# Three engines held to one written order in the first stage of a two-layer transformer step

## The chip, the cores and the metric

The kernel runs on one core of a Trainium2 chip. The metric is the device time of one execution, in microseconds. The text says PE for TensorE, DVE for VectorE, ACT for ScalarE, POOL for GpSimd and SP for SyncE, as the profile does; each takes its own instructions in their order in the program.

## The reference

Two layers (neighbourhood attention, then a gated linear recurrence), each with a feed-forward network, on 640 tokens (512 latent, 128 context) of width 1024. Each sub-layer begins with an RMS norm that is modulated by a conditioning vector; the change lies in the first one and in the first product behind it.

```python
def _adaln(cond, w_mod, b_mod):
    m = jax.nn.silu(cond) @ w_mod + b_mod
    return jnp.split(m, N_MOD, axis=-1)

def _modulate(x, g, shift, scale):
    return _rms_norm(x, g) * (1 + scale[:, None, :]) + shift[:, None, :]

xm_l = _modulate(lat, norm_g[i, 0], sh1_l, sc1_l)   # with cond = c; context tokens: cond = c_ctx
q_l, k_l, v_l = _qkv(xm_l, attn_w_qkv[j])
```

## The kernel before

Activations lie with their features on partitions: eight tiles `k` = 0 to 7 of 128 features by 640 tokens (`KT` = 8). A product in float32 accuracy is made of three matmuls in a faster format: each operand is split into a high part (a cast on ACT) and a low part (value less high part, on DVE), and high·high, low·high and high·low are summed in one bank of PSUM. `split` (L1061 to L1063) does this for a tile, `unit` (L166 to L181) for a weight tile that it also loads.

The first stage is `start`. SP issues its loads in one queue: eight tiles of `x`, 16 tiles of the first modulation weights (`sw`, 512 KB each: group `g` of two tiles `k`, scale `j` = 1 or shift `j` = 0, half `h`), and in between the query and the key weights of the first head pair (`raw` from `wqk`, L313). Behind them follow the value weights (`raw` from `wv`, L170), the conditioning vectors spread over all partitions (`csb`, L1127) and more.

Then, in this order of dependence:

- The statistic: ACT squares, DVE sums to `ssq`, `moment` lets PE sum over partitions (L390), DVE and POOL make the inverse root (L392, L394), DVE writes it on diagonals (L399) and PE spreads it over all partitions (L402), ACT copies it to `rsb` (L403), the latent 512 columns and the context 128 apart.
- The adaLN vectors, `vectors(g)`: PE multiplies a piece (L327, 16 passes for one `g` and `j`), DVE (`j` = 1) or ACT (`j` = 0) copies the row (L328), four small matmuls select the columns (L334) and four small DVE instructions finish the factors `A` and shifts `B` of two tiles (L339, L340).
- The scaling, `scaled(k, A, B)`. An even tile: DVE multiplies by `A` and `rsb` (L350), ACT adds `B` into the high part (L351), DVE makes the low part (L352), each for the latent and the context columns. An odd tile: POOL multiplies it by `rsb` beforehand (L369), ACT scales and shifts it (L348), then `split`.
- The products, `products(k)`: 12 matmuls (L362 to L364) on two weights (query, key) and two chunks of 320 tokens, into four banks that collect all eight `k`.

What runs behind the stage starts with `qk(0, ...)`, which empties those four banks, and `vq(0, ...)`, whose matmuls L228 to L230 take the value weights (split by L180 on ACT and L181 on DVE).

The order on each engine isn't that of the code: a scheduler with its own estimates of durations chooses it under the dependences, so instructions of several groups `g`, and of what follows the stage, lie mixed.

Of the kernel before, what the change touches and what calls it, by code (L numbers as in the profile page):

```python
# [9 lines left out]
F32 = mybir.dt.float32  # L10
F32R = mybir.dt.float32r
# [114 lines left out]
class _Step:  # L126
# [161 lines left out]
    def start(self, hi, lo, sp, big):  # L288
# [14 lines left out]
        for g in range(KT // NB):  # L303
            for j in (1, 0):
                for h in range(2):
                    w = self.t([P, 4, n], F32, f"sw{g}{j}{h}", 1, sp)
                    nc.sync.dma_start(w, self.i["wm0"][j, g, h])
                    parts[g, j, h] = w
            if g == 1:
                raws = []  # L310
                for f in (0, KT):
                    raw = self.t([P, KT, P], F32, "raw", 3)
                    nc.sync.dma_start(raw, self.i["wqk"][f])  # L313
                    raws.append(raw)
# [3 lines left out]
            if k:  # L318
                nc.vector.tensor_tensor(ssq, ssq, q, ALU.add)

        def vectors(g):
            pm = {j: self.ps("sp") for j in (1, 0)}
            row = idle[:, g % 2 * 2 * n:g % 2 * 2 * n + 2 * n]
            for j in (1, 0):
                for h in range(2):
                    for k4 in range(4):
                        nc.tensor.matmul(pm[j][32 * k4:32 * k4 + 32, 0:n], csp[:, 4 * h + k4], parts[g, j, h][:, k4], start=(h == 0), stop=(h == 1))  # L327
                (nc.vector.tensor_copy if j else nc.scalar.copy)(row[:, j * n:j * n + n], pm[j][:, 0:n])  # L328
            out = []
            pt = self.ps("tp")  # L330
            for j in (1, 0):
                for kb in range(NB):
                    q = NB * j + kb
                    nc.tensor.matmul(pt[:, 2 * q:2 * q + 2], row[:, q * P:q * P + P], sel, start=True, stop=True)  # L334
            for kb in range(NB):
                k = g * NB + kb
                A = self.t([P, 2], F32, "a0", 4, sp)
                B = self.t([P, 2], F32, "b0", 4, sp)
                nc.vector.tensor_scalar(A, pt[:, 2 * (NB + kb):2 * (NB + kb) + 2], b1[:, k:k + 1], self.col("ng00", k), ALU.add, ALU.mult)  # L339
                nc.vector.tensor_scalar(B, pt[:, 2 * kb:2 * kb + 2], self.col("bsh", k), None, ALU.add)  # L340
                out.append((k, A, B))
            return out

        def scaled(k, A, B):
            for s, a, b in _pieces(0, NTOK):
                v = self.x[:, k, a:b]
                if k % 2:
                    nc.scalar.activation(v, v, AF.Identity, scale=A[:, s:s + 1], bias=B[:, s:s + 1])  # L348
                else:
                    nc.vector.scalar_tensor_tensor(v, v, A[:, s:s + 1], self.rsb[:, a:b], ALU.mult, ALU.mult)  # L350
                    nc.scalar.activation(hi[:, k, a:b], v, AF.Identity, bias=B[:, s:s + 1])  # L351
                    nc.vector.scalar_tensor_tensor(lo[:, k, a:b], v, B[:, s:s + 1], hi[:, k, a:b].bitcast(F32), ALU.add, ALU.subtract)  # L352
            if k % 2:
                self.split(hi[:, k, 0:NTOK], lo[:, k, 0:NTOK], self.x[:, k, 0:NTOK])

        acc = [[self.pg(), self.pg()], [self.pg(), self.ps("op")]]

# [5 lines left out]
                    nc.tensor.matmul(ps, wl[:, k], hi[:, k, s], start=False, stop=False)  # L363
                    nc.tensor.matmul(ps, wh[:, k], lo[:, k, s], start=False, stop=(k == KT - 1))  # L364

        vec = vectors(0)
        self.moment(ssq, sp)
        for k in range(1, KT, 2):
            nc.gpsimd.tensor_tensor(self.x[:, k], self.x[:, k], self.rsb, ALU.mult)  # L369
        for g in range(1, KT // NB + 1):  # L370
            todo = vec
            for t in todo:
                scaled(*t)
            if g < KT // NB:
                vec = vectors(g)
            if us is None:
                us = []
                for raw in raws:
                    u = [self.t([P, KT, P], F32R, m, 3) for m in ("whi", "wlo")]
                    self.split(*u, raw)  # L380
                    us.append(u)
            for t in todo:
                products(t[0])
        return acc

    def moment(self, ssq, sp):
# [5 lines left out]
        nc.vector.tensor_scalar(v, ps[:, 0:NT], 1.0 / D, EPS, ALU.mult, ALU.add)  # L392
        r = self.t([P, 8], F32, "rs", 2)[:, 0:NT]
        nc.gpsimd.tensor_tensor(r, v, self.mhalf.broadcast_to([P, NT]), ALU.pow)  # L394
        dg = self.t([P, NT, P], F32, "dg", 1, sp)
        self.rsb = self.t([P, NTOK], F32, "rsb", 1, sp)
        for s, a, b in _pieces(0, NTOK):
            j, m = a // P, (b - a) // P
            nc.vector.tensor_tensor(dg[:, j:j + m], self.ident.unsqueeze(1).broadcast_to([P, m, P]), r[:, j:j + m].unsqueeze(2).broadcast_to([P, m, P]), ALU.mult)  # L399
            ps = self.ps("sp" if s == 0 else "tp")  # L400
            for q in range(j, j + m):
                nc.tensor.matmul(ps[:, (q - j) * P:(q - j) * P + P], self.ones, dg[:, q], start=True, stop=True)  # L402
            nc.scalar.copy(self.rsb[:, a:b], ps[:, 0:b - a])  # L403

    def square(self, k, t0, t1):
        nc = self.nc
# [658 lines left out]
    def lru_gate(self, f, hi, lo, lp):  # L1065
# [152 lines left out]
```

## Time and profile before

| | |
|---|---|
| median of 3 runs | 1559.95 us (1559.09 to 1560.55) |
| the profiled execution: time | 1561.15 us |
| its span, first to last instruction | 1559.4 us |
| PE, DVE, ACT, POOL busy | 1491.8, 1079.1, 717.9, 208.9 us |
| DMA, mean over the span | 121 GB/s |

A timeline row gives the start, the length, the engine, the line, the operation, the tile written and the tiles read, a count of merged instructions, and in brackets the idle time before it with what ended it. A row of a group gives the count, then busy time and mean duration, then the idle time before its instructions. PEld are weight loads, SPq is a DMA issue. The pages count times from the span's start.

### The profile page before, as it was taken

The numbers are of one execution on the slowest core, as the hardware profiler recorded it, in microseconds if no ns is written. First come the engines' busy times: TensorE is split into PE (matmuls) and PEld (weight loads), VectorE is DVE, ScalarE is ACT, GpSimd is POOL, SyncE is SP. The second block draws the span as 40 slices with busy tenths as digits, with TensorE's granted clock in tenths as the row PEclk, the third lists the DMA queues.
The fourth block names the chain that finished last, engine by engine and source line by source line (L and its number), as shares of the span: only waits on it lengthen the run. The fifth ranks groups of instructions, "written<-read, shape, count | busy, mean of one in ns | idle before, by whom it ended". The sixth has DMA issues, their size and how long they took to land.

```text
span 1559.4 us, 26024 instructions
## 1 busy us (share of the span) xinstructions
PE 1491.8 (96%) x10303; PEld 1444.5 (93%) x10303; DVE 1079.1 (69%) x2042; ACT 717.9 (46%) x1326; POOL 208.9 (13%) x230
## 2 busy tenths in 40 slices
PE   5999999989999999999999999969999999999996
PEld 3899999879999999999999887869999999999996
DVE  5678688859899996444446489875876665556545
ACT  4676667654332123212334499754634342524231
POOL 2111122100111110000000000000132323232300
PEclk9999999989999999999999999989999999999997
DMA  9545555536566663222223112134242231313111
GB/s 377 157 131 170 159 167 168 145 118 200 176 191 188 209 207 100 73 82 82 62 83 113 62 62 68 55 108 153 68 132 80 70 109 55 109 55 108 55 55 68
DMA packets 69753, 188.25 MB, mean 121 GB/s; under 512 B 7792, under 2 KB 23296, under 8 KB 69504
## 3 DMA queue, kind: packets, MB, share of 16 engines
q1 hardware_dynamic: 57824, 144.49, 29.2%
q0 software_dynamic: 11520, 41.95, 8.8%
q8 instruction: 81, 1.33, 0.3%
q14 instruction: 40, 0.33, 0.1%
q10 hardware_dynamic: 288, 0.16, 0.0%
HBM read 171.09 MB, written 8.92 MB: 115 GB/s over the span
## 4 chain that ended last, share of the span: by engine, by line
PE 82%; ACT 7%; DVE 7%; issue 3%; DMA 1%; POOL 0%; DVEq 0%; ACTq 0%; POOLq 0%
PE mm L213 13%; PE mm L212 13%; PE mm L214 13%; PE mx L212 5%; PE mx L213 5%; PE mx L214 5%; PE mx L825 3%; PE mx L827 3%; PE mx L826 3%; PE op L671 2%; PE tp L595 2%; PE mc L825 1%; PE mc L826 1%; PE mc L827 1%; PE mm L228 1%
## 5 line engine op out<-in xcount | busy, mean ns | idle before, releaser
L212 PE MATMUL mm<-big,whi 128*128 128x320 f32 (+2 forms) x1251 | 389.9, 314 | 15.3 <-ACT big L1062 9.2
L213 PE MATMUL mm<-big,whi 128*128 128x320 f32 (+2 forms) x1251 | 391.4, 313 | 4.3 <-DVE big L1063 4.0
L214 PE MATMUL mm<-big,wlo 128*128 128x320 f32 (+2 forms) x1251 | 390.6, 313 | 0.0
L212 PEld LDWEIGHTS mm<-big,whi 128*128 128x128 f32 x1251 | 237.1, 190 | 18.4 <-ACT big L1062 10.0
L213 PEld LDWEIGHTS mm<-big,whi 128*128 128x128 f32 x1251 | 238.1, 190 | 6.3 <-DVE big L1063 5.4
L214 PEld LDWEIGHTS mm<-big,wlo 128*128 128x128 f32 x1251 | 237.7, 190 | 1.1
L242 DVE SCALAR_TENSOR_TENSOR mprod<-mraw,csb 128x1024 f32<-128x1024 f32 x160 | 195.4, 1221 | 7.2 <-DMA mraw<-in_wm 6.5
L180 ACT CAST whi<-raw 128x1024 fp32r<-128x1024 f32 (+1 forms) x87 | 90.2, 1037 | 131.3 <-PE mm L213 77.2
L462 DVE SCALAR_TENSOR_TENSOR x<-mm,G,x 128x192 f32<-128x192 f32 (+3 forms) x211 | 84.6, 434 | 91.2 <-PE mm L214 90.2
L181 DVE TENSOR_TENSOR wlo<-raw,whi 128x1024 fp32r<-128x1024 f32 (+1 forms) x87 | 105.9, 1218 | 29.1 <-ACT whi L180 26.1
L214 PE MATMUL mm<-big,wlx 128*128 128x320 f32 (+3 forms) x362 | 112.3, 310 | 0.0
L213 PE MATMUL mm<-big,whx 128*128 128x320 f32 (+3 forms) x362 | 112.1, 310 | 0.0
L212 PE MATMUL mm<-big,whx 128*128 128x320 f32 (+3 forms) x362 | 112.1, 310 | 0.0
L238 POOL DMA_DIRECT2D mraw<-in_wm x80 | 43.2, 540 | 381.4 <-DVE mprod L242 268.4
L212 PE MATMUL mx<-big,whi 128*128 128x320 f32 (+3 forms) x285 | 90.1, 316 | 0.9 <-DVE big L680 0.9
L213 PE MATMUL mx<-big,whi 128*128 128x320 f32 (+3 forms) x285 | 89.6, 314 | 0.0
L214 PE MATMUL mx<-big,wlo 128*128 128x320 f32 (+3 forms) x285 | 89.4, 314 | 0.0
L432 POOL TENSOR_TENSOR rs<-var,mhalf 128x3 f32<-128x3 f32 (+1 forms) x8 | 7.7, 961 | 569.1 <-DVE var L430 569.1
L180 ACT CAST whx<-raw 128x1024 fp32r<-128x1024 f32 (+1 forms) x39 | 40.0, 1027 | 89.5 <-PE mm L213 53.3
L212 PE MATMUL mx<-big,whx 128*128 128x320 f32 (+3 forms) x246 | 76.5, 311 | 0.0
L213 PE MATMUL mx<-big,whx 128*128 128x320 f32 (+3 forms) x246 | 76.3, 310 | 0.0
L214 PE MATMUL mx<-big,wlx 128*128 128x320 f32 (+3 forms) x246 | 76.3, 311 | 0.0
(300 smaller groups left out, 3691.4 us busy)
## 6 DMA issues: line engine op xcount, KB each, us to landing
raw<-in_gu SPq DMA_DIRECT2D x88, 512.0 KB, 3.5
mraw<-in_wm POOLq DMA_DIRECT2D x80, 512.0 KB, 4.0
raw<-in_dn SPq DMA_DIRECT2D x24, 512.0 KB, 3.6
sw<-in_wm SPq DMA_DIRECT2D x16, 512.0 KB, 10.1
raw<-in_wqk SPq DMA_DIRECT2D x16, 512.0 KB, 3.7
raw<-in_wi SPq DMA_DIRECT2D x16, 512.0 KB, 3.5
raw<-in_dn SPq DMA_DIRECT2D x16, 448.0 KB, 3.3
raw<-in_wv SPq DMA_DIRECT2D x8, 512.0 KB, 4.0
```

The source lines that it names most:

```text
L180: nc.scalar.copy(hi, raw)
L181: nc.vector.tensor_tensor(lo, raw, hi.bitcast(F32), ALU.subtract)
L212: nc.tensor.matmul(ps, hi[:, k], xhi[:, k, s], start=(k == 0), stop=False)
L213: nc.tensor.matmul(ps, hi[:, k], xlo[:, k, s], start=False, stop=False)
L214: nc.tensor.matmul(ps, lo[:, k], xhi[:, k, s], start=False, stop=(k == nk - 1))
L238: nc.gpsimd.dma_start(w, self.i["wm"][l * 6 + j - 2, f])
L242: nc.vector.scalar_tensor_tensor(prod, w, 1.0, self.csb[:, s], ALU.mult, ALU.mult, accum_out=out[:, s, f:f + 1])
L462: self.nc.vector.scalar_tensor_tensor(xs, ps[:, a - t0:b - t0], G[:, s, f:f + 1], xs, ALU.mult, ALU.add)
L595: nc.tensor.transpose(tp[:, j * P:j * P + P], s[:, j * P:j * P + P], self.ident)
L825: nc.tensor.matmul(ps, hi[:, k], xh[:, k], start=start and k == 0, stop=False, skip_group_check=not start)
L826: nc.tensor.matmul(ps, hi[:, k], xl[:, k], start=False, stop=False, skip_group_check=not start)
L827: nc.tensor.matmul(ps, lo[:, k], xh[:, k], start=False, stop=(k == KH - 1), skip_group_check=not start)
```

## The change

- `vectors(g)` falls into `piece(g, j)` (one piece and the copy of its row) and `select(g)`; `moment` ends with the diagonals, and `spread(s)` does the rest for one of the two column ranges.
- The query and key weights are loaded behind the first four `sw` tiles instead of eight. Their split falls into `weight(j)` (ACT) and `rest(j)` (DVE).
- `scaled` takes an even and an odd tile together and issues the steps of both in a fixed sequence.
- `in_order` adds dependences without a wait, so that PE, DVE and ACT each take the stage's instructions in the order of the code. Instructions from behind the stage may still be put in between.

```diff
-            if g == 1:
+            if g == 0:
                 raws = []
                 for f in (0, KT):
                     raw = self.t([P, KT, P], F32, "raw", 3)
...
+            lat, ctx = (0, a0, a1), (1, p0, p1)
+            for step, part in ((gain, lat), (gain, ctx), (whole, lat), (high, lat), (high, ctx), (whole, ctx), (low, lat), (low, ctx)):
+                step(*part)
+            self.split(hi[:, m, 0:NTOK], lo[:, m, 0:NTOK], self.x[:, m, 0:NTOK])
...
-        vec = vectors(0)
-        self.moment(ssq, sp)
-        for k in range(1, KT, 2):
-            nc.gpsimd.tensor_tensor(self.x[:, k], self.x[:, k], self.rsb, ALU.mult)
-        for g in range(1, KT // NB + 1):
-            todo = vec
-            for t in todo:
-                scaled(*t)
-            if g < KT // NB:
-                vec = vectors(g)
...
-            for t in todo:
-                products(t[0])
+        def pieces(g):
+            piece(g, 1)
+            piece(g, 0)
+
+        def ready(g):
+            scaled(*select(g))
...
+        us = []
+        with self.in_order(mybir.EngineType.PE, mybir.EngineType.DVE, mybir.EngineType.Activation):
+            piece(0, 1)
+            self.moment(ssq, sp)
+            piece(0, 0)
+            weight(0)
+            self.spread(0, sp)
+            todo = select(0)
+            self.spread(1, sp)
+            for k in range(1, KT, 2):
+                nc.gpsimd.tensor_tensor(self.x[:, k], self.x[:, k], self.rsb, ALU.mult)
+            rest(0)
+            weight(1)
+            scaled(*todo)
+            rest(1)
+            for step, i in ((products, 0), (pieces, 1), (products, 1), (ready, 1), (pieces, 2), (products, 2), (ready, 2), (products, 3)):
+                step(i)
+            piece(3, 1)
+            products(4)
+            piece(3, 0)
+            for step, i in ((products, 5), (ready, 3), (products, 6), (products, 7)):
+                step(i)
...
+    @contextmanager
+    def in_order(self, *engines):
+        code = self.nc.cur_bb.bb.instructions
+        n = len(code)
+        yield
+        last = {}
+        for ins in list(code)[n:]:
+            if ins.engine in engines:
+                if ins.engine in last:
+                    self.tc.add_manual_dep(ins, last[ins.engine], mybir.DependencyInfo(mybir.DependencyClass.NoSync, mybir.DependencyReason.DATA), reason="in_order")
+                last[ins.engine] = ins.name
```

PE at the stage's start, before: `sw` 20 and 21 are the first piece, 22 and 23 the second, L334 the selection, L390 the statistic, L402 its spread.

```order
L327 MATMUL sp_170<-sw_20_115,csp_99 32x256 x4
L327 MATMUL sp_170<-sw_21_117,csp_99 32x256 x4
L327 MATMUL sp_171<-sw_22_119,csp_99 32x256 x4
L334 MATMUL tp_190<-sel_102,big_84 128x2 x2
L390 MATMUL tp_203<-ones_72,ssq_106 128x1 x5
L327 MATMUL sp_171<-sw_23_121,csp_99 32x256 x4
L334 MATMUL tp_190<-sel_102,big_84 128x2 x2
L402 MATMUL sp_216<-dg_213,ones_72 128x128 x4
```

The same place now (L423 was L390, L440 was L402, L337 was L334):

```order
L327 MATMUL sp_170<-sw_20_115,csp_99 32x256 x4
L327 MATMUL sp_170<-sw_21_117,csp_99 32x256 x4
L423 MATMUL tp_180<-ones_72,ssq_106 128x1 x5
L327 MATMUL sp_194<-sw_22_119,csp_99 32x256 x4
L327 MATMUL sp_194<-sw_23_121,csp_99 32x256 x4
L440 MATMUL tp_207<-dg_190,ones_72 128x128 x4
L337 MATMUL tp_213<-sel_102,big_84 128x2 x4
L440 MATMUL tp_226<-dg_190,ones_72 128x128
```

The statistic stands one `sw` tile and half a selection earlier, and the selection behind the first spread.

ACT around the cast of the value weights, L180, before. `b_62` and `a_61` belong to tile 3, `b_73` and `a_72` to tile 5, `b_71` to tile 4:

```order
L348 ACTIVATE big_98<-big_98,b_62_270,a_61_269 128x512
L348 ACTIVATE big_98<-big_98,b_62_270,a_61_269 128x128
L351 ACTIVATE big_85<-big_98,b_60_266 128x512
L351 ACTIVATE big_85<-big_98,b_60_266 128x128
L1062 CAST big_85<-big_98 128x640
L328 COPY big_84<-sp_316 128x256
L348 ACTIVATE big_98<-big_98,b_73_345,a_72_344 128x512
L348 ACTIVATE big_98<-big_98,b_73_345,a_72_344 128x128
L180 CAST whi_512<-raw_510 128x1024
L351 ACTIVATE big_85<-big_98,b_71_341 128x512
L351 ACTIVATE big_85<-big_98,b_71_341 128x128
```

And now (`b_66`, `a_65`: tile 3, `b_64`: tile 2; L357 was L348, L360 was L351, L1100 was L1062, L329 was L328, L1178 was L1128):

```order
L1100 CAST big_85<-big_98 128x640
L329 COPY big_84<-sp_270 128x256
L180 CAST whi_512<-raw_510 128x1024
L357 ACTIVATE big_98<-big_98,b_66_302,a_65_301 128x512
L360 ACTIVATE big_85<-big_98,b_64_298 128x512
L360 ACTIVATE big_85<-big_98,b_64_298 128x128
L357 ACTIVATE big_98<-big_98,b_66_302,a_65_301 128x128
L1178 ACTIVATE csb_81<-csb_81 128x2048
L1100 CAST big_85<-big_98 128x640
L329 COPY big_84<-sp_325 128x256
```

L180 has moved from tiles 4 and 5 to ahead of tiles 2 and 3, and the activation of `csb` from tiles 6 and 7 to ahead of the cast of tile 3.

PE around the last selection, before (`tp_402`), with the blocks of tiles 4 to 6 mixed:

```order
L327 MATMUL sp_383<-sw_36_147,csp_99 32x256 x4
L327 MATMUL sp_383<-sw_37_149,csp_99 32x256 x4
L334 MATMUL tp_402<-sel_102,big_84 128x2 x2
L362 MATMUL mm_166<-big_85,whi_273 128x320
L363 MATMUL mm_166<-big_85,wlo_274 128x320
L362 MATMUL mm_168<-big_85,whi_277 128x320
L363 MATMUL mm_168<-big_85,wlo_278 128x320
```

And now (`tp_426`), between the last matmul of tile 5 and the first of tile 6:

```order
L376 MATMUL op_169<-big_85,whi_234 128x320
L377 MATMUL op_169<-big_85,wlo_235 128x320
L378 MATMUL op_169<-big_86,whi_234 128x320
L337 MATMUL tp_426<-sel_102,big_84 128x2 x4
L376 MATMUL mm_166<-big_85,whi_204 128x320
L377 MATMUL mm_166<-big_85,wlo_205 128x320
```

The selection stood ahead of products of tiles that were scaled before it; now the products of the tiles that it serves come directly behind it.

On DVE the subtraction for the value weights (L181, behind L180) now stands between the multiplications and the low parts of tile 2, and each copy of an adaLN row stands behind the subtraction of the odd tile before it. On ACT behind the stage, the copies that empty the first bank (`mm_166`) come first now; before, the cast of the second value weights and the copies of two other banks stood ahead of them. The scheduler also places other instructions behind the stage otherwise, through the attention part.

More of the change, by code (lines that the diff above doesn't have):

```diff
@@ L319, in start, with piece, select @@
                 nc.vector.tensor_tensor(ssq, ssq, q, ALU.add)
[L321 to L328, printed above, removed]
+        pm, rows = {}, {}
+        def piece(g, j):
+            pm[g, j] = ps = self.ps("sp")
+            for h in range(2):
+                for k4 in range(4):
+                    nc.tensor.matmul(ps[32 * k4:32 * k4 + 32, 0:n], csp[:, 4 * h + k4], parts[g, j, h][:, k4], start=(h == 0), stop=(h == 1))
+            rows[g, j] = row = idle[:, (g % 2 * 2 + j) * n:(g % 2 * 2 + j) * n + n]
+            (nc.vector.tensor_copy if j else nc.scalar.copy)(row, ps[:, 0:n])
+        def select(g):
             out = []
```

54 lines of the change are left out of this document (30 added, 24 removed).

## The prediction, on record before the run

> **What bounds the kernel now.** I read the chain that ended last first, then the busy times by stretch, then the timeline of the first 54 us, the groups by line of that stretch, and last the DMA issues. The chain is mostly TensorE:
>
> ```profile
> PE 82%; ACT 7%; DVE 7%; issue 3%; DMA 1%; POOL 0%; DVEq 0%; ACTq 0%; POOLq 0%
> ```
>
> Busy times by stretch, the columns being length, then PE, PEld, DVE, ACT and POOL busy, granted clock, DMA share, GB/s:
>
> ```profile
> 20.00:27.00 7.00, 6.41 (x43) 3.59 (x44) 4.79 (x11) 3.25 (x5) 1.00 (x1) 0.52 1.03 418
> 27.00:30.50 3.50, 3.15 (x35) 1.92 (x35) 3.50 (x6) 2.00 (x5) 3.50 (x3) 1.00 1.01 401
> 30.50:40.00 9.50, 8.41 (x61) 6.94 (x62) 5.96 (x13) 3.70 (x7) 2.44 (x2) 1.00 0.95 388
> 40.00:51.50 11.50, 11.03 (x89) 9.62 (x89) 7.93 (x19) 8.48 (x13) 5.03 (x9) 1.00 0.56 154
> 70.00:1560.00 1490.00, 1439.63 (x9896) 1402.96 (x9894) 1037.15 (x1951) 680.18 (x1263) 193.61 (x208) 0.98 0.37 113
> ```
>
> After 70 us PE is busy 1439.6 of 1490 us, so a microsecond that the first stage wins or loses there reaches the end, unless one of the few later waits takes it up. Inside the stage PE is not idle for long either: from 30.5 to 51.5 us it is busy 19.4 of 21 us. What the new order can still win is therefore mainly in front of 30.5 us, and what it can lose is the density behind it. The landmarks of the stage, from the timeline:
>
> ```profile
> 15.51 1.08 PE L327 MATMUL sp<-sw,csp 128*32 128x256 f32 x8 [0.21 <-DMA sw<-in_wm]
> 16.99 1.25 PE L390 MATMUL tp<-ones,ssq 128*128 128x1 f32 x10
> 18.53 1.19 POOL L394 TENSOR_TENSOR rs<-var,mhalf 128x5 f32<-128x5 f32 x1 [17.00 <-DVE var L392]
> 20.59 2.05 PE L402 MATMUL sp<-dg,ones 128*128 128x128 f32 x8 [0.68 <-DVE dg L399]
> 24.24 1.23 DVE L1063 TENSOR_TENSOR wlo<-raw,whi 128x1024 fp32r<-128x1024 f32 x1 [0.20 <-ACT whi L1062]
> 26.00 6.94 POOL L369 TENSOR_TENSOR big<-big,rsb 128x640 f32<-128x640 f32 x4 [6.29 <-ACT rsb L403]
> 26.37 2.34 DVE L1063 TENSOR_TENSOR wlo<-raw,whi 128x1024 fp32r<-128x1024 f32 x1
> 29.08 1.07 PE L327 MATMUL sp<-sw,csp 128*32 128x256 f32 x16
> 30.53 0.41 PE L362 MATMUL mm<-big,whi 128*128 128x320 f32 x1 [0.37 <-ACT big L351]
> 33.02 0.41 DVE L328 COPY big<-sp 128x256 f32<-128x256 f32 x1
> 33.48 0.61 PE L334 MATMUL tp<-sel,big 128*128 128x2 f32 x4 [1.06 <-DVE big L328]
> ```
>
> and its end, from the same view of PE alone:
>
> ```profile
> 50.60 0.31 PE L362 MATMUL mm<-big,whi 128*128 128x320 f32 x1
> 50.74 0.31 PE L363 MATMUL mm<-big,wlo 128*128 128x320 f32 x1
> ...
> 51.64 0.31 PE L364 MATMUL op<-big,whi 128*128 128x320 f32 x1
> 53.63 0.39 PE L228 MATMUL mm<-whi,big 128*128 128x256 f32 x1 [1.68 <-ACT r L522]
> ```
>
> One product matmul follows the other at 0.147 us, so a block of 12 (one k) is 1.76 us. An adaLN piece of 16 passes is 1.07 us. A hand-over from one engine to the next is about 0.05 us (the copy ends at 33.43, the matmul starts at 33.48). The stage ends at 51.95, and its successor L228 starts at 53.63. That start is my yardstick.
>
> **The front.** The statistic's matmuls (L390) move from behind the third adaLN tile to behind the second, so from 16.99 to where L327 now starts that third tile, about 15.4: 1.6 us. The power on POOL, the diagonal and the first spread follow, at most 2 us earlier, and POOL's four products start at about 22 instead of 26.0. The two query and key weights are loaded four transfers earlier; their splits no longer wait for the transfer. The second split (L1063) moves behind the whole scaling of pair 0, 1. While POOL multiplies, that DVE instruction took 2.34 us against 1.23, and pair 0, 1's five DVE operations now all fall into those 7 us. So block 0 finishes between 27 (nothing slowed) and 32 (all of it slowed), and I take 31. Behind it come two pieces (2.1), block 1 (1.8) and the selection (0.6): 35.5, or 31.5 at best. Neither value matters, for the reason that follows.
>
> **The wait that is added.** On ScalarE the cast of the value weights (L180, whi from raw) now stands ahead of all of pair 2, 3's steps. Before, it stood in pair 4, 5:
>
> ```profile
> 41.54 1.03 ACT L180 CAST whi<-raw 128x1024 fp32r<-128x1024 f32 x1
> ```
>
> Its transfer keeps its place in the queue, behind the 16 adaLN tiles and two weights:
>
> ```profile
> 25.61 0.33 SPq L170 DMA_DIRECT2D raw<-in_wv  x1
> ```
> ```profile
> raw<-in_wv SPq DMA_DIRECT2D x1, 512.0 KB, 10.6
> ```
> ```profile
> 26.89 0.33 SPq L1127 DMA_DIRECT2D csb<-in_cc  x1
> ```
> ```profile
> csb<-in_cc SPq DMA_DIRECT2D x1, 1024.0 KB, 11.8
> ```
>
> It lands at 25.6 + 10.6 = 36.2, csb at 38.7. The bytes ahead of both are the same as before, and the DMA share is 0.95 to 1.03 in every stretch from 20 to 40, so no order on the other engines brings them forward. ScalarE is a queue: everything of pair 2, 3 waits there until 36.2, however early the front was. Queued behind the cast are pair 2, 3's four steps, and for them wait the subtractions on DVE and block 2 on PE.
>
> The prices, by line of ScalarE and of VectorE in the first 51.6 us (count, then busy us and mean ns):
>
> ```profile
> L348 ACT ACTIVATE big<-big,b,a 128x512 f32<-128x512 f32 (+1 forms) x8 | 4.8, 648 | 4.7 <-DVE b L340 4.3 <-POOL big L369 0.3
> L351 ACT ACTIVATE big<-big,b 128x512 fp32r<-128x512 f32 (+1 forms) x8 | 4.2, 553 | 1.5 <-DVE big L350 1.5
> L1062 ACT CAST big<-big 128x640 fp32r<-128x640 f32 x4 | 2.8, 712 | 0.0
> L1128 ACT ACTIVATE csb<-csb 128x2048 f32<-128x2048 f32 x1 | 1.9, 1912 | 0.0
> L180 ACT CAST whi<-raw 128x1024 fp32r<-128x1024 f32 x1 | 1.0, 1027 | 0.0
> ```
> ```profile
> L1063 DVE TENSOR_TENSOR big<-big,big 128x640 fp32r<-128x640 f32 x4 | 3.3, 818 | 0.0
> L339 DVE TENSOR_SCALAR a<-tp,b,cols 128x2 f32<-128x2 f32 x8 | 2.2, 271 | 3.5 <-PE tp L334 3.5
> L181 DVE TENSOR_TENSOR wlo<-raw,whi 128x1024 fp32r<-128x1024 f32 x1 | 1.2, 1226 | 0.1
> ```
> ```profile
> 46.11 1.00 DVE L350 SCALAR_TENSOR_TENSOR big<-big,a,rsb 128x512 f32<-128x512 f32 x2
> ...
> 48.14 1.01 DVE L352 SCALAR_TENSOR_TENSOR big<-big,b,big 128x512 fp32r<-128x512 f32 x2 [1.02 <-ACT big L351]
> ```
>
> From 36.2 the steps add up so; of the pairs of latent and context instructions I give the latent one 0.7 to 0.75 and the context one the rest.
>
> - Pair 2, 3: cast to 37.2, the odd tile's latent part to 37.9, the even one's high part to 38.6. Block 2 starts at 38.6. On DVE L181 (1.2) stands ahead of its low parts, which end at 39.6, so the block ends at about 40.9.
> - ScalarE goes on with two context parts (39.6), then the activation of csb, whose data are there (41.5), and only then pair 2, 3's last cast (42.2). Its subtraction on DVE is done at 43.0, and the copy of the next adaLN row is queued behind it: 43.4. The selection of pair 4, 5 waits for that row, and on PE everything waits behind the selection: PE stands idle from 40.9 to 43.5. It ends at 44.1.
> - Block 3 to 45.9 and a piece to 46.9 cover the scaling of pair 4, 5: four small DVE instructions (0.75, by the 0.27 of L339), 1.0 for L350's pair, 0.7 and 0.75 for the first high and low part, 47.1. Block 4 ends at 48.8, the last piece at 49.9, block 5 at 51.6, the last selection at 52.2.
> - Nothing stands between that selection and block 6, so the same scaling is in the open: 53.0, 53.75, 54.45 for the first high part, 55.2 for the low one. Block 6 ends at 56.9. Pair 6, 7's cast is done at 56.1 and its subtraction at 56.9. Block 7 ends at 58.7.
> - Some 20 hand-overs at 0.05 are 1.0: 59.7.
>
> **What is given back at the end.** L228 waited 1.68 us for ScalarE to empty its bank. Now the bank's own three matmuls come first in block 7, over a microsecond before the block ends, and ScalarE empties that bank first. I take the wait as gone: L228 at 59.7. If it stayed, 1.7 are to be added. Other instructions behind the stage are reordered too, up to about 300 us; their waits of 1 to 2.5 us each (the largest in that stretch) can move either way, which I take as nothing and keep as 2 us either side in the range.
>
> **The sum.** 59.7 less 53.63 is 6.1 us, rounded to 6. The profiled execution took 1561.15 us, span 1559.4 and 1.75 around it. It lies 1.2 above the median of the runs, 1559.95. The forecast is 1567.2 beside the former and 1566.0 beside the latter.
>
> **The clock, row and rule.** The granted clock was 0.52 in the stretch from 20 to 27 and 1.00 in those from 27 on. By these rows alone the new order would be past the slow time at 27, and nothing is added. The Trainium skill (TensorE: Matmul & The Clock Gate, What's actually happening) says that the clock halves after an idle window of about 3.4 us, and is full again only after a busy one. It is a rival with its own result below.
>
> **The rivals.**
> - **The half clock lasts.** In the new order PE has little to do from 21.5 to 31, because block 0 waits for its factors. If the clock then returns only after some 3 us of dense work, the rest of block 0, the two pieces and a part of block 1, 1.5 to 3 us of work at full speed, take twice that. The selection of pair 2, 3 ends at 37 to 38.5, its small factors are there at 37.8 to 39.3, and ScalarE starts on the pair then instead of at 37.2: 0.6 to 2.1 more, and as much again where block 0 is late. The time is 1568. For it: from 20 to 27 PE was busy 6.4 of 7 us with small matmuls and had half the clock all the same. Against it: the clock was back at 27, behind adaLN pieces and spreads alone. The sentence of the skill above speaks for it: by that rule the time is this 1568.
> - **Dense PE, faster.** If ScalarE meets its cast with the data there, nothing holds pair 2, 3. Blocks 1 to 7 (12.3), six pieces (6.4), three selections (1.8) and the one open scaling (2.3) are 22.8; from a block 0 that ends at 28 the stage ends at 50.8, L228 follows at once, 2.8 earlier than now: 1557.2. It decides at the landing of the value weights: by 33 there is no wait, at 36.2 there is. For it: L180's group shows no idle time before it (0.0), though that is at 41.5. Against it: the two rows that say 36.2.
> - **Given back later.** PE's waits behind the stage could take up the delay, since some end on transfers or on DVE work that the stage doesn't set. In 1490 us PE lacks 50 us of busy time, so 3 to 5 us could vanish in there: 1561 to 1563, no difference. Against it: most of these waits end on work that PE itself fed.
>
> **How the numbers follow.** The forecast has 0.55, the half clock 0.17, given back 0.14, dense PE 0.14. A measurement here tells apart about 0.2%, 3.1 us. Slower by more: the first two less a little, 0.71. Within: 0.15. Faster by more: 0.14, though 1557.2 is only just there. The range leaves out dense PE and the upper tail: the low end is 1559 (given back, with 2 us of reordering in its favour), the high end 1571 (half clock, with a bit of reordering against). The forecast's own range is 1563 to 1569.
>
> **What would show it.** Right: in the changed trace ScalarE idles up to about 36.2 and ends that wait on the transfer of the value weights; PE waits 2 to 3 us at the selections of pair 4, 5 and at the first matmul of block 6; L228 starts near 59.7 without the wait of 1.68. Wrong: ScalarE reaches the cast after its data by more than 2 us, or the last product ends before 53. If the stage ends near 60 and the time is still about 1560, the later waits took it up.

## The result, and the profile after

The changed kernel takes 1569.45 us (median of 6 runs, 1566.56 to 1576.8) against 1558.65 (6 runs, 1553.89 to 1560.55) of the kernel before on the same chip: a ratio of 1.0082, 95% interval 1.0055 to 1.0109, that is 8.6 to 17.0 us more, with 12.8 in the middle (the ratio is one of means; the medians lie 10.8 apart). The forecast was +6. The direction was right, the size was half of it. The profiled execution took 1569.67 us, with a span of 1567.9.

The busy times of the changed kernel by the same stretches (length; PE, PEld, DVE, ACT, POOL busy; granted clock; DMA share; GB/s):

```profile
20.00:27.00 7.00, 2.79 (x19) 2.60 (x19) 4.76 (x7) 3.91 (x6) 4.04 (x3) 0.81 1.03 410
27.00:30.50 3.50, 2.10 (x6) 1.30 (x7) 3.50 (x4) 1.51 (x3) 3.06 (x2) 0.50 1.03 412
30.50:40.00 9.50, 8.53 (x57) 5.62 (x57) 2.00 (x3) 1.32 (x2) 0.00 (x0) 0.61 0.96 391
40.00:51.50 11.50, 8.96 (x72) 7.09 (x76) 7.49 (x19) 7.20 (x12) 0.00 (x0) 0.86 0.51 152
51.50:70.00 18.50, 13.94 (x96) 11.83 (x97) 8.69 (x15) 6.01 (x15) 6.60 (x10) 0.81 0.17 58
```

Before, PE had the full clock from 27 on; now it is at 0.50 to 0.61 up to 40, and lower than full in both stretches behind that. PE is "busy" 8.53 of 9.5 us from 30.5 to 40, and does 57 matmuls there: busy at half the speed. Its landmarks, from the timeline of PE (L376 to L378 are the products, L337 the selection):

```profile
26.78 0.63 PE L376 MATMUL mm<-big,whi 128*128 128x320 f32 x1 [4.21 <-ACT big L360]
32.13 0.64 PE L377 MATMUL mm<-big,wlo 128*128 128x320 f32 x1 [0.97 <-DVE wlo L393]
33.76 3.64 PE L327 MATMUL sp<-sw,csp 128*32 128x256 f32 x32
39.50 0.95 PE L337 MATMUL tp<-sel,big 128*128 128x2 f32 x8
42.78 0.41 PE L376 MATMUL mm<-big,whi 128*128 128x320 f32 x1 [0.47 <-ACT big L360]
47.14 1.05 PE L337 MATMUL tp<-sel,big 128*128 128x2 f32 x8 [1.43 <-DVE big L329]
48.87 0.47 PE L376 MATMUL mm<-big,whi 128*128 128x320 f32 x1
57.33 0.95 PE L337 MATMUL tp<-sel,big 128*128 128x2 f32 x8
60.62 0.41 PE L376 MATMUL mm<-big,whi 128*128 128x320 f32 x1 [2.33 <-ACT big L360]
64.19 0.63 PE L378 MATMUL mm<-big,whi 128*128 128x320 f32 x1 [1.99 <-DVE big L363]
69.11 0.28 PE L228 MATMUL mm<-whi,big 128*128 128x256 f32 x1
```

A product matmul of 0.31 is one at full clock, and the next starts 0.147 us later; one of 0.47 is at half clock, with 0.267 to the next. The two pieces (32 passes) take 3.64 where two cost 2.1 before. L228 starts at 69.11 without a wait: 15.5 us later than before, where the forecast had 6.1. The queue of ScalarE around the cast of the value weights (L180):

```profile
37.47 0.37 ACT L329 COPY big<-sp 128x256 f32<-128x256 f32 x1 [8.74 <-PE sp L327]
37.74 1.05 ACT L180 CAST whi<-raw 128x1024 fp32r<-128x1024 f32 x1
41.30 0.82 ACT L357 ACTIVATE big<-big,b,a 128x512 f32<-128x512 f32 x1 [2.51 <-DVE b L343]
43.31 1.90 ACT L1178 ACTIVATE csb<-csb 128x2048 f32<-128x2048 f32 x1
```

The cast doesn't wait for its transfer. ScalarE waits 8.74 us for the adaLN piece ahead of it and 2.51 for the factors behind it: the late front, not the transfer, sets pair 2, 3. VectorE and GpSimd at the stage's end (L363 is the low part of an even tile, for 512 and 128 columns; L1174 and L674 are memsets, L238 issues transfers, L681 adds a mask: set-up work of the attention behind the stage):

```profile
58.96 1.00 DVE L353 SCALAR_TENSOR_TENSOR big<-big,a,rsb 128x512 f32<-128x512 f32 x2
60.60 3.54 DVE L363 SCALAR_TENSOR_TENSOR big<-big,b,big 128x512 fp32r<-128x512 f32 x2 [0.63 <-ACT big L360]
```
```profile
59.11 1.84 POOL L1174 MEMSET KZ<- 64x960 f32 x2 [29.06 <-PE tp L337]
60.90 0.56 POOL L674 MEMSET bt<- 128x256 f32 x2
61.41 1.29 POOL L238 DMA_DIRECT2D mraw<-in_wm  x2
62.72 3.07 POOL L681 TENSOR_TENSOR bt<-bt,mask 128x256 f32<-128x256 f32 x4
```

L363's pair takes 1.01 with GpSimd idle (L352's row before); beside GpSimd's set-up work it takes 3.54, and PE's wait of 1.99 ends on it.

Behind the stage the delay shrinks: 15.5 us at L228's first, 10.8 at its last (270.2 before, 281.0 now), 8.5 at the end of the span. These are single executions; by the ratio 12.8 arrive at the end, so 2.7 of the 15.5 vanish. So three things were to be explained: where the stage's 9.4 us above the forecast come from, why a part of them vanishes later, and which of the held orders is to blame.

### The profile page after: what moved, and what is told of

It is laid out like the page before. It is cut to its first block, busy times and chain, and to the rows that moved or that the text cites. A ratio compares the mean times of both kernels' runs of the same rounds, so it can differ in the third digit from the quotient of the medians.

```text
span 1567.9 us, 26026 instructions
## 1 busy us (share of the span) xinstructions
PE 1495.7 (95%) x10303; PEld 1448.6 (92%) x10303; DVE 1085.1 (69%) x2042; ACT 718.0 (46%) x1326; POOL 205.9 (13%) x230
## 4 chain that ended last, share of the span: by engine, by line
PE 84%; DVE 7%; ACT 6%; issue 2%; POOL 0%; DMA 0%; DVEq 0%; ACTq 0%; POOLq 0%
PE mm L213 13%; PE mm L212 13%; PE mm L214 13%; PE mx L212 5%; PE mx L214 5%; PE mx L213 5%; PE mx L863 3%; PE mx L865 3%; PE mx L864 3%; PE op L709 2%; PE tp L633 2%; PE mc L863 1%; PE mc L864 1%; PE mc L865 1%; PE mm L229 1%
## 5 line engine op out<-in xcount | busy, mean ns | idle before, releaser
L180 ACT CAST whi<-raw 128x1024 fp32r<-128x1024 f32 (+1 forms) x87 | 90.3, 1038 | 121.2 <-PE mm L213 69.9
L181 DVE TENSOR_TENSOR wlo<-raw,whi 128x1024 fp32r<-128x1024 f32 (+1 forms) x87 | 105.3, 1211 | 27.7 <-ACT whi L180 25.0
L238 POOL DMA_DIRECT2D mraw<-in_wm x80 | 43.0, 538 | 377.0 <-DVE mprod L242 276.6
L180 ACT CAST whx<-raw 128x1024 fp32r<-128x1024 f32 (+1 forms) x39 | 40.0, 1027 | 90.4 <-PE mm L213 52.5
```

Source lines behind the costliest of these rows:

```text
L180: nc.scalar.copy(hi, raw)
L181: nc.vector.tensor_tensor(lo, raw, hi.bitcast(F32), ALU.subtract)
L238: nc.gpsimd.dma_start(w, self.i["wm"][l * 6 + j - 2, f])
```

## The experiments

A ratio is that to the kernel before, run beside it on the same chip (x1 to x3 ran on another chip than x4 to x6); 0.001 is 1.56 us, and an interval of these runs is about 2.5 us to either side. L228 stands for the stage's end, with its distance from the 53.6 of the kernel before; it is read from one execution of each kernel. All kernels but the last six leave the order behind the stage to the scheduler.

The theory to begin with was that of the prediction: the stage waits for ScalarE's cast and csb's activation and for the open scaling, and what the stage loses reaches the end. The rival was the half clock; a second one GpSimd.

### e1_cast, e2_cast_warm: the cast late, then filler on PE

The value weights' cast and csb's activation go, on ScalarE, behind what the written order has up to block 3.

```diff
             for step, i in ((products, 0), (pieces, 1), (products, 1), (ready, 1), (pieces, 2), (products, 2), (ready, 2), (products, 3)):
                 step(i)
+            self.cut = self.last(mybir.EngineType.Activation)
...
+            with tc.issue_after(self.cut):
                 self.vq(0, xhi, xlo, V)
...
                 nc.scalar.activation(self.csb, self.csb, AF.Silu)
```

> The changed kernel, with the cast of the value weights and the activation of csb put behind pair 4, 5's last cast on ScalarE. Theory on record (ScalarE's place for these two decides): pair 2, 3 no longer waits, L228 starts 4 to 5 us before the changed kernel's 69.1, at 64 to 65, and the time falls by as much. Rival (half clock and POOL decide): in the changed trace the cast ran at 37.7 without waiting for its data, so only the 1.9 us of csb and the 1.2 us of the subtraction behind the cast go; L228 at 67 to 68, the time 1 to 2 us lower.

e1_cast: ratio 1.0123 (1.0100 to 1.0146), L228 at 65.7 (+12.1). The stage ends 3.4 us earlier than in the changed kernel, and the time isn't lower: both branches expected it to fall. The second kernel adds, to this one, matmuls that feed nothing (9 behind the second spread, 2 ahead of the selection of pair 4, 5, 2 behind that of pair 6, 7; the diff shows only what one call adds):

```diff
+        def warm(n):
+            for _ in range(n):
+                nc.tensor.matmul(self.ps("sp"), self.ones, ssq[:, 0:512], start=True, stop=True)
```

> As e1_cast, and PE gets matmuls that compute nothing used: 9 of 128x512 between the spread and block 0, 2 behind block 2, 2 behind the last selection. Rival (half clock): the granted clock is 1.00 from 20 us to the last low part, the first two pieces take 2.1 instead of 3.6 us, block 3 takes 1.8 instead of 3.2; L228 starts 4 to 6 us before that of e1_cast and the time is 2 to 5 us below that of e1_cast. Theory on record (clock adds nothing): the added matmuls only cost, L228 0 to 2 us later than in e1_cast.

e2_cast_warm: 1.0029 (1.0012 to 1.0046), L228 at 61.5 (+7.9). More work on PE, and 0.94% less time: the clock matters, and the prediction's "nothing is added" falls. Whether the cast costs stayed open: its stage gained, its time didn't.

### e3_pool: GpSimd's set-up work behind the stage

The memsets (L1174) wait for `done`, the stage's last VectorE instruction; the rest of GpSimd's work is queued behind them. The attention of the first two head pairs and the query and key products behind it are placed behind the memsets too (`tc.issue_after(z)`, left out of this diff and those below), so the edit also touches the later order.

```diff
+            self.done = self.last(mybir.EngineType.DVE)
...
-                nc.gpsimd.memset(self.kz[HD - a * HD:P - a * HD, a].bitcast(F32), 0.0)
+                z = nc.gpsimd.memset(self.kz[HD - a * HD:P - a * HD, a].bitcast(F32), 0.0).ins
+                tc.add_manual_dep(z, self.done.name, mybir.DependencyInfo(mybir.DependencyClass.Sync, mybir.DependencyReason.DATA), reason="kz")
```

> The changed kernel, with POOL's instructions behind the stage (KZ, bt, their loads and additions) made to wait for the last subtraction of the stage on VectorE. Rival (POOL holds VectorE at the end): the last low part takes 1.0 instead of 3.5 us, PE's wait of 2.0 in block 6 goes and with it the half clock of blocks 6 and 7, L228 at 64 to 65.5 instead of 69.1. Theory on record (POOL plays no part there): L228 stays at 69, the time within 1 us of the changed kernel or above.

1.0084 (1.0061 to 1.0107), L228 at 65.4 (+11.8). L363's pair is back at 1.01, the stage ends 3.7 us earlier, and the time is that of the changed kernel. Twice now an earlier end of the stage brought nothing: something behind it differed.

### e5_all: the three edits together

```diff
+            with tc.issue_after(self.cut):
...
+                tc.add_manual_dep(z, self.done.name, mybir.DependencyInfo(mybir.DependencyClass.Sync, mybir.DependencyReason.DATA), reason="kz")
...
+            warm(9)
```

> The changed kernel with all three repairs together: the cast of the value weights and the activation over 2,048 numbers behind the stage's steps, GpSimd's set-up work behind the stage's last VectorE instruction, and the 9, 2 and 2 filler matmuls. If the half clock and the late cast are what the stage pays (GpSimd's set-up came too late to meet the last subtraction once the clock was full): L228 starts within 1 us of the kernel with cast and filler (61.5), time 1562 (+4 to +6 on the kernel before). If GpSimd's set-up still costs time of its own behind the stage: L228 the same, time 1564 to 1566. If it was still in the stage's way: L228 at 59 to 60 and 1559 to 1560.

1.0046 (1.0030 to 1.0062), L228 at 61.6 (+8.0), as in e2_cast_warm; the time, +7.2, is above the +4 to +6 expected, by less than the noise. With the clock full, GpSimd's set-up was no longer in the stage's way. The best held order still ends 8 us late.

### e4_free, e7_pe, e8_dve_act: which order costs

All three are the changed kernel, code and sequence, with fewer engines held; the new lines are those of e4_free, e7_pe and e8_dve_act:

```diff
-        with self.in_order(mybir.EngineType.PE, mybir.EngineType.DVE, mybir.EngineType.Activation):
+        with self.in_order():
+        with self.in_order(mybir.EngineType.PE):
+        with self.in_order(mybir.EngineType.DVE, mybir.EngineType.Activation):
```

> The changed code with the dependences of in_order left out, so that the scheduler mixes again; earlier statistic, earlier query and key weights and the divided steps stay. If holding the order is what costs (blocks of 12 with nothing mixed in): PE finds work in every wait, L228 at 50 to 54, the time at that of the kernel before or 1 to 3 us below. If the new code itself costs (POOL's products beside all of pair 0, 1's steps, the half clock in front of block 0): L228 at 58 or later, the time 3 us or more above the kernel before.

> The changed kernel with TensorE alone held to the written order; VectorE and ScalarE are ordered by the scheduler. If TensorE's order (no products to fill its waits) is what costs: idle gaps and half clock stay, L228 at 60 to 66, time 1564 to 1570 (+6 to +12). If the order on VectorE and ScalarE is what costs (the cast, the copies behind the subtractions): L228 at 56 to 58, time 1556 to 1559.

> The changed kernel with VectorE and ScalarE held and TensorE free, so that the scheduler mixes adaLN pieces and products of two blocks. If TensorE's order is what costs: matmuls at the full clock through the stage's middle (spacing of L376 to L378 at 0.15 us), L228 at 56 to 58, time within 0.3% of the kernel before (1555 to 1561). If the order of the two feeding engines is what costs: L228 at 62 or later, time 1564 to 1570.

e4_free: 0.9995 (0.9978 to 1.0012), L228 at 56.1 behind the old wait of 1.68, between the two branches expected (54 at most, 58 at least). e7_pe: 1.0093 (1.0077 to 1.0109), L228 at 62.7. e8_dve_act: 1.0096 (1.0081 to 1.0110), L228 at 63.5. With nothing held, the rest of the change (early statistic, early weights, finer steps), together with the later order that the scheduler then chose, is worth nothing that can be measured. Holding either side puts L228 9 to 10 us later than in the kernel before, and 6.6 to 7.4 later than in e4_free, the same code with nothing held. In each expectation the branch that cleared the held side failed; the other has L228 right, and its time, 1570 at most, is passed by 3 to 4 us. Timeline rows of PE, of e4_free, e7_pe and e8_dve_act:

```profile
31.06 0.47 PE L378 MATMUL op<-big,whi 128*128 128x320 f32 x1
...
50.62 0.41 PE L376 MATMUL mm<-big,whi 128*128 128x320 f32 x1 [2.72 <-ACT big L360]
...
56.09 0.39 PE L228 MATMUL mm<-whi,big 128*128 128x256 f32 x1 [1.68 <-ACT r L560]
```
```profile
57.43 0.63 PE L376 MATMUL mm<-big,whi 128*128 128x320 f32 x1 [2.72 <-ACT big L360]
57.86 0.47 PE L377 MATMUL mm<-big,wlo 128*128 128x320 f32 x1
```
```profile
59.22 0.63 PE L378 MATMUL mm<-big,whi 128*128 128x320 f32 x1 [1.03 <-DVE big L363]
59.65 0.47 PE L378 MATMUL op<-big,whi 128*128 128x320 f32 x1
```

Free, PE has its last product at half clock at 31.06, and the open scaling (2.72) comes at 50.62 and is followed by the full clock. Held on either side, block 6 comes 5 to 7 us later (57.43, and 55.63 in e8_dve_act), and the half clock is back: for block 6 in e7_pe (up to 60.8), for most of blocks 6 and 7 in e8_dve_act. The order isn't all of that: PE waits the same 2.72 ahead of block 6 in e4_free, at full clock behind it, and in e7_pe, at half. The times of the two are higher still than their stages explain: +14.5 and +15 for +9 to +10. A wait behind the attention, the largest of PE from 325 to 400 us in e7_pe, isn't among those of the kernel before in that stretch:

```profile
PE mm L212 <- DVE x L500: 3.9, 1, 3.9
PE tp L633 <- ACT S L628: 1.9, 2, 1.5
```

### e6_delay: a late start alone

The kernel before, with idle work of PE between the stage and L228 (`late` is at first the stage's last matmul):

```diff
+        with self.tc.issue_after(late):
+            for _ in range(29):
+                self.late = nc.tensor.matmul(self.ps("sp"), self.ones, ssq[:, 0:512], start=True, stop=True).ins
...
-            self.vq(0, xhi, xlo, V)
+            with tc.issue_after(self.late):
+                self.vq(0, xhi, xlo, V)
```

> The kernel before, with 29 matmuls of 128x512 that do nothing useful put between the stage's last product and L228: 29 x 0.592 = 17.2 us, less the wait of 1.68 that they cover, so that L228 starts 15.5 us later, as it does in the changed kernel, but with TensorE dense. If the later program gives back about half of any late start (waits that were there before take it up): +8 to +9 us at the end, 1565 to 1567, the same as the changed kernel. If what the changed kernel gave back comes from its own order of work in the attention part: +13 to +16, 1570 to 1573.

1.0161 (1.0141 to 1.0181), L228 at 78.0. I had taken 0.592 for one of these matmuls; the row shows two passes for each and 25 us for all:

```profile
53.48 25.05 PE L387 MATMUL sp<-ssq,ones 128*128 128x512 f32 x58
77.97 0.68 PE L228 MATMUL mm<-whi,big 128*128 128x256 f32 x1
```

So the delay is 24.3, and 25.1 us (22 to 28) arrive at the end, with this kernel's own later order in it: no sign that a late start is given back as such. Up to here the end against L228 was +12.8 for +15.5, +19 for +12.1, +13 for +11.8, +14.5 for +9.1: no line. The scheduler orders the whole program, and a change in the stage had given every kernel another order behind it.

### x1_after_lb, x2_before_la, x3_warm_lb: the later order held fixed

A table, made from the built kernels, gives each engine's sequence of the 13,000 instructions behind the stage, and dependences without a wait put it in force; the stage itself is not touched:

```diff
                 acc = self.start(xhi, xlo, sp, wbig)
+            n0 = len(nc.cur_bb.bb.instructions)
...
+        code = list(self.nc.cur_bb.bb.instructions)[n0:]
...
+                ins = own[j + at]
+                if prev is not None:
+                    self.tc.add_manual_dep(ins, prev.name, mybir.DependencyInfo(mybir.DependencyClass.NoSync, mybir.DependencyReason.DATA), reason="later")
+                prev = ins
```

> The changed kernel's first stage, and behind it every engine's instructions in the order that they have in the kernel before (a table of 13,000 places; the scheduler had given the two kernels different later orders). If the give-back of some 5 us in the changed kernel comes from its own later order: it goes, L228 at 69 and the time 12 to 16 us above the kernel before (1570 to 1575). If a late start is given back whatever the order: as the changed kernel, +8 to +10 (1566 to 1569).

> The other way round: the first stage of the kernel before (L228 at 53.6), and behind it every engine's order of the changed kernel. If the later order is worth the 5 us by itself: 1551 to 1555, faster than both kernels. If the later order is worth nothing by itself: 1557 to 1561, the same as before.

> The first stage with the late cast and the filler matmuls (L228 at 61.5, +7.9), and behind it the order of the kernel before. If only the stage's end counts once the later order is fixed: +7 to +9 (1565 to 1567), against +4.5 for the same stage with its own later order. If the end follows the stage by half: +4 (1562 to 1563).

x1_after_lb: 1.0094 (1.0077 to 1.0111), L228 at 70.5 (+16.9). x2_before_la: 0.9983 (0.9971 to 0.9996), L228 at 53.6. x3_warm_lb: 1.0043 (1.0028 to 1.0058), L228 at 61.6 (+8.0). With the old later order the changed stage costs 14.7 us, and the changed kernel's later order is worth 2.6 us (0.6 to 4.5) even behind the old stage: that version is faster than both kernels, by a little. The waits go with the order, not with the stage. PE's largest waits from 70 to 400 us, first x1_after_lb (stage changed, order old), then x2_before_la (stage old, order changed):

```profile
PE tp L683 <- ACT S L678: 2.0, 2, 1.5
PE mm L263 <- DVE big L1151: 1.6, 1, 1.6
PE sp L665 <- DMA KS<-KS: 1.4, 2, 0.8
```
```profile
PE tp L643 <- ACT S L638: 4.2, 2, 3.3
PE tp L671 <- DVE S L670: 1.4, 1, 1.4
PE mx L260 <- DVE big L728: 0.9, 1, 0.9
PE sp L625 <- DMA KS<-KS: 0.9, 1, 0.9
```

The columns are line waited at and releaser, us in total, times, longest. The 1.6 on a low part belongs to the old order (it was among the waits of the kernel before, as was one of 2.4 on the transfer KS, here 1.4 and 0.9); the 4.2 and 1.4 in the softmax belong to the new one (the changed kernel has both). All waits of this view add up to 10.4 before and 10.0 in x1_after_lb, 7.2 in the changed kernel and 8.3 in x2_before_la: 1.7 to 3.2 us less with the changed order, which is about what it gains.

### x4_fill_lb, x5_pool_lb, x6_cast_lb: the three causes, one at a time

The same three edits as in e2_cast_warm (the filler alone), e3_pool and e1_cast, each on x1_after_lb; in x4_fill_lb the other engines are held by the table in the stage too, so that only PE's clock differs, and the time that the filler itself takes.

```diff
             self.spread(1, sp)
+            warm(9)
...
+                tc.add_manual_dep(z, self.done.name, mybir.DependencyInfo(mybir.DependencyClass.Sync, mybir.DependencyReason.DATA), reason="kz")
...
+            with tc.issue_after(self.cut):
```

> The changed kernel's stage with the 9, 2 and 2 filler matmuls alone; ScalarE, VectorE, GpSimd and the queues are held to exactly the order of the kernel with the changed stage and the later order of the kernel before, so that only TensorE's clock differs from it. If the half clock costs what its slow stretches show (pieces 1.5, block 3 1.4, blocks 6 and 7 2.2, selections 0.5, with what waits for them): L228 5 to 7 us earlier (62 to 65), time 5 to 7 us lower than the 1572 of that kernel (1565 to 1567). If the waits of the order set the pace at any clock: L228 within 2 us of 69, 1570 to 1572.

> The changed kernel's stage with GpSimd's set-up work (two memsets, DMA issues, mask additions) held until the stage's last VectorE instruction has run; later order as in the kernel before. If the collision on the last subtraction costs its 2 to 2.5 us: L228 2 to 2.5 us earlier at the same clock (66 to 67, or 65.4 as in the kernel with its own later order), time 1569 to 1570. If the late set-up costs as much behind the stage: L228 the same, 1571 to 1573.

> The changed kernel's stage with the cast of the value weights and the activation over 2,048 numbers behind the stage's steps up to block 3; later order as in the kernel before. If these two on ScalarE, and the subtraction that follows the cast on VectorE, cost what the profile shows in front of the third selection (the wait of 1.43 and more): L228 at 65 to 67, time 1568 to 1570, and not 1575.6 as with its own later order, whose excess would so be the order's. If the late cast itself costs time behind the stage: 1574 to 1577.

| kernel | L228 | against before | ratio (interval) | us by the ratio |
|---|---|---|---|---|
| x1_after_lb | 70.5 | +16.9 | 1.0094 (1.0077 to 1.0111) | +14.7 |
| x5_pool_lb | 67.3 | +13.7 | 1.0090 (1.0073 to 1.0107) | +14.0 |
| x6_cast_lb | 66.6 | +13.0 | 1.0072 (1.0055 to 1.0088) | +11.2 |
| x4_fill_lb | 62.2 | +8.6 | 1.0051 (1.0031 to 1.0072) | +8.0 |
| x3_warm_lb | 61.6 | +8.0 | 1.0043 (1.0028 to 1.0058) | +6.7 |

In one later order the end follows the stage, to within 2.2 us. L228 here includes a wait of 0.64 to 1.10 for its bank. The clock is worth 6.7 us (2.5 to 11 with both intervals), the late cast 3.5 (0 to 7); together (x3_warm_lb) they are worth 8.0, which the runs can't tell from their sum or from the clock alone. The edits aren't separate causes either: in x6_cast_lb PE waits only 0.20 at the third selection, and block 3 runs at full clock (its products start 0.15 apart), so a part of the 3.5 is the clock. GpSimd's set-up work shows at L228 (3.2 us, some of it again clock: the last half clock lasts 3.4 us in x5_pool_lb and 6.8 in x1_after_lb) and not in the time (0.7, anything from a loss of 3 to a gain of 4): whether it costs is not settled. x6_cast_lb also tells where the 1.0123 of e1_cast came from: the same stage edit is at 1.0072 in the old order, with L228 at 66.6, so the excess was its later order.

PE in x4_fill_lb (L447 the filler, L380 the pieces, L390 the selection, L429 to L431 the products, L281 what was L228):

```profile
21.92 7.89 PE L447 MATMUL sp<-ssq,ones 128*128 128x512 f32 x18
31.64 0.41 PE L430 MATMUL mm<-big,wlo 128*128 128x320 f32 x1 [0.80 <-DVE wlo L450]
32.56 1.93 PE L380 MATMUL sp<-sw,csp 128*32 128x256 f32 x32
36.32 0.95 PE L390 MATMUL tp<-sel,big 128*128 128x2 f32 x8
39.60 0.41 PE L429 MATMUL mm<-big,whi 128*128 128x320 f32 x1 [0.47 <-ACT big L413]
62.22 0.39 PE L281 MATMUL mm<-whi,big 128*128 128x256 f32 x1 [1.09 <-ACT r L618]
```

and ScalarE at the cast (here L233):

```profile
34.56 0.37 ACT L382 COPY big<-sp 128x256 f32<-128x256 f32 x1 [6.33 <-PE sp L380]
35.15 1.05 ACT L233 CAST whi<-raw 128x1024 fp32r<-128x1024 f32 x1 [0.21 <-DMA raw<-in_wv]
38.12 0.82 ACT L410 ACTIVATE big<-big,b,a 128x512 f32<-128x512 f32 x1 [1.93 <-DVE b L396]
```

Filled, PE takes the two pieces in 1.93 instead of the changed kernel's 3.64 and starts block 2 at 39.60 instead of 42.78. The filler itself costs about 1 us, ahead of the third selection (44.93), whose row was copied by 43.9; at blocks 0 and 6 PE still waits behind it (0.80 and 0.51). So the 6.7 are what the clock costs less that. Even now the cast waits 0.21 us for its transfer, and ScalarE then waits 1.93 for the factors.

## Why the size was wrong, step by step

- **The failed step: the clock.** "By these rows alone the new order would be past the slow time at 27, and nothing is added." The rows were those of an order in which PE was busy 6.41 of the 7 us from 20 to 27; in the new one it is busy 2.79, idle for 4.21 in one piece; by the recorded clock the half clock begins in that gap, at 24.3, and lasts to 38.0. The half clock came back twice, for block 3 and for blocks 6 and 7. What it costs was shown by x4_fill_lb against x1_after_lb: 6.7 us where the forecast had none. The rival "the half clock lasts" had the mechanism, with the chance 0.17 and, for the first stretch alone, 2 us. The Trainium skill (TensorE: Matmul & The Clock Gate, What's actually happening) gives an idle window of about 3.4 us as what halves the clock. The trace agrees in part: the gap ahead of block 0 is longer, 4.21, but the recorded clock falls 1.7 us into it, and block 3 was at half clock behind an idle stretch of 1.43 us and small matmuls.
- **The front: "Neither value matters."** It did. Block 0 and the pieces ended not at 31 and 33.1 but at 33.8 and 37.4, and pair 2, 3 began when its factors came, at 41.3. The forecast held it back by the transfer's landing at 36.2 and had the selection done by 35.5. The landing itself was well estimated (35.15 in x4_fill_lb); it was never the last thing waited for. So the forecast's largest step, that ScalarE idles for this transfer, failed as well: by that landing, 10.2 us behind the issue, the cast started about 2 us behind its data. With the clock full, the factors are still 1.93 us later than the cast. That the forecast's 59.7 is near the 61.1 at which the products of x4_fill_lb end is therefore partly luck: the late factors took the place of a transfer wait of which 0.21 was left.
- **Right in kind, too large: the wait ahead of the third selection.** Forecast 2.6 us (40.9 to 43.5) for csb's activation, the last cast, its subtraction and the copied row; PE waits 1.43 there, on that row. Moving the two ScalarE instructions away takes it to 0.20 and is worth 3.5 us (0 to 7) in x6_cast_lb, block 3 at full clock included.
- **Right: the open scaling.** 2.25 us (52.2 to 54.45) were forecast between the last selection and block 6; the row says 2.33.
- **Right: L228's wait of 1.68** is gone in the changed kernel, whose bank is emptied earlier. It is no gift of the stage, though: with the old later order 0.64 to 1.10 of it are back.
- **Not foreseen: GpSimd's set-up work** beside the last subtractions, 2.5 us in the row of L363. Its part in the time isn't settled.
- **Given back later.** "Their waits … can move either way, which I take as nothing and keep as 2 us either side": measured, 2.6 us in the change's favour, by the order and not by slack that takes up a delay (e6_delay, and the table of the last six).

The sum closes: 8.0 for the held order at full clock (forecast 6.1), 6.7 for the clock, less 2.6 for the later order, is 12.1, against 12.8 (8.6 to 17.0) measured. The first two are the 14.7 of x1_after_lb split in two, so the check lies in the last term: x1_after_lb less the changed kernel gives 1.9 for the later order, x2_before_la 2.6, and the first can't be told from nothing. What the 8.0 are made of, beside the filler's own 1 us, is read from rows, not tried: the front, the wait at the third selection, the open scaling.

## What to carry to other kernels

A written order that leaves PE nothing to do while one chain is on its way paid twice here, for the gap and for the half clock behind it; before holding an order, look for stretches where it thins PE's work, and cost the work behind them at both clocks. Where a scheduler orders the whole program, an edit in one place reshuffles all that follows: to price the edit, fix the later order first, or the reshuffle, worth here from -2.6 us (x2_before_la) to +8.0 (e1_cast against x6_cast_lb), is read as the edit's effect. A transfer's landing sets a wait only if everything else ahead of it is early.

## What the runs showed of the hardware

- The recorded clock can miss a half clock. In e3_pool the column says 1.00 from 30.5 to 40, while the product matmuls take 0.47 and start 0.27 apart, as at half clock, up to 35. The durations are the surer sign.

```profile
30.50:40.00 9.50, 8.37 (x54) 5.45 (x55) 3.35 (x4) 1.32 (x2) 0.90 (x1) 1.00 0.92 375
```
```profile
33.91 0.47 PE L378 MATMUL mm<-big,whi 128*128 128x320 f32 x1
34.18 0.47 PE L376 MATMUL op<-big,whi 128*128 128x320 f32 x1
```

- The clock falls late: in x5_pool_lb the last dense work ends at 57.1, block 6 begins at full clock at 60.40, and the half clock comes at about 61.7, in the midst of dense products, and stays until 65.1.
- The clock changes on a grid. Slices of 0.1 us of the changed kernel (the column behind the busy times is the mean clock) put its changes at 24.32, 37.97, 48.21 and 51.63, further ones at 61.87 and 68.69:

```profile
24.30:24.40 0.10, 0.00 (x0) 0.00 (x0) 0.10 (x1) 0.00 (x0) 0.10 (x1) 0.60 1.23 492
37.90:38.00 0.10, 0.10 (x2) 0.10 (x1) 0.00 (x0) 0.10 (x1) 0.00 (x0) 0.64 0.60 246
48.20:48.30 0.10, 0.10 (x1) 0.10 (x2) 0.07 (x1) 0.00 (x0) 0.00 (x0) 0.56 0.67 113
51.60:51.70 0.10, 0.10 (x4) 0.00 (x0) 0.00 (x0) 0.10 (x1) 0.00 (x0) 0.87 0.00 0
```

They lie 13.65, 10.24, 3.42, 10.24 and 6.82 apart, that is 4, 3, 1, 3 and 2 times 3.41; in x5_pool_lb the same way 13.65, 10.24, 3.41, 10.24 and 3.42. So what a gap costs depends also on where it falls between two such marks, which fits the two fates of the 2.72 us in e4_free and e7_pe; that was not tried by an experiment.
- VectorE beside GpSimd: the pair of 512 and 128 columns that takes 1.01 alone took 3.13 beside GpSimd's products (L353 and L363 from 24.0 to 30.2) and 3.54 beside its transfer issues and mask additions, but 1.01 beside the memset alone (x4_fill_lb, L416 at 56.82 while the memset ran from 56.44 to 58.28).
